# One streaming encoder step: the last whole gate chunks also go into pairs of half products

## The chip, the core and the metric

The kernel runs on one core of a Trainium2 chip. The metric is the device time of one launch in microseconds (us), as the median of three runs. The engines named below are TensorE (PE in the profile; PEld is its weight loads), VectorE (DVE), ScalarE (ACT), GpSimd (POOL) and SyncE (SP, which here only issues DMAs).

## What is computed

Two layers work on 640 tokens (512 of a prompt, 8 x 16 of running streams). Cut to what matters here, a layer is:

```
(a_u, a_v, a_g, b_x, b_g, c_q, c_kv, c_kr, c_g, m_q, gate_logits) = split_cols(x @ w_in)
oa = gmlp(a_u, a_v) * silu(a_g)              # branch A
ob = rglru(conv4(b_x)) * silu(b_g)           # branch B, a recurrence over the tokens
oc = mla(c_q, c_kv, c_kr) * silu(c_g)        # branch C
om = mem_attend(m_q, mem_k, mem_v)           # branch M
g = sigmoid(gate_logits).reshape(B, T, 4, D_MODEL)
merged = g[0]*(oa @ w_a) + g[1]*(ob @ w_b) + g[2]*(oc @ w_c) + g[3]*(om @ w_m)
x = layer_norm(ALPHA * x + merged @ w_out)
```

`gate_logits` has 4 x 1024 columns. With 128 columns to a chunk that is 32 gate chunks in each layer, eight for each branch.

## The kernel before

Every float32 operand of a product is split into a high and a low part (ACT casts the high one, DVE subtracts to get the low one), and a product takes three passes: high by high, high by low, low by high. There are two ways to compute a chunk of 128 columns of `x @ w_in` for all 640 tokens:

- **Whole** (`fm_chunk`, line 121 in the profile, tile `fm`): 8 blocks of the inner dimension x 3 passes x 2 halves of the tokens, 48 matmuls of 128x128 by 320.
- **In pairs** (`Pair`, `run_pair`, `product`, line 423, tiles `fp_a`, `fp_b`, `fp_c`): two chunks together are a 2x2 block product, done by a scheme with seven half products of 12 matmuls each, 84 in all. It needs sums of weight blocks (DVE, line 369), sums of blocks of x (the `xt` tiles, made early in the layer, put in DRAM and brought back by `x_sums_back`, line 356), and some additions of results (line 372). `on()` keeps the operations of the pairs in a fixed order on each engine.

A gate chunk is followed by tanh (ACT) and the branch's product `y` (`merge_y`, 24 matmuls, tile `y`, line 121), which DVE multiplies by the gate and adds to `macc`.

The recurrence of branch B is worked in four chunks c of 128 channels. For each: `lru_in(c)` (a whole chunk `fm`, its copy out of PSUM into `lb[c % 2]`, and a convolution on DVE, line 994), `lru_split(c)` (splits the result into the one tile `lx`, and loads and splits the gate weights `lru_w`), `lru_gates(c)` (12 matmuls, tile `gate`, line 1015, and two tanh) and `lru_rest(c)` (about ten dependent operations on DVE, ACT and POOL, with the scan on line 1036). There are only two `lb` buffers, so `lru_in(3)` can't copy its chunk out of PSUM until `lru_rest(1)` is done.

The end of a layer runs so: `lru_in` and `lru_gates(0)`, `lru_rest(0)` between the four steps of `mem_prompt` (branch M's attention, tiles `ms_ps`, `ptm_ps`, `mo_ps`); then `merge_whole` with the first four gate chunks of branch A, computed whole, written by hand between `lru_gates(1)` to `lru_rest(3)`; then `merge_pairs` with 14 pairs for the other 28 gate chunks; then the output projection (`y_ps`).

Buffers come from pools by tag, and all tiles of a tag share its slots. The ones at issue: `acc` in PSUM, **2** slots of two banks, used by `fm`, `gate`, `y` and `fp_a`; `raw`, 3 slots, every weight load; `t` (`tmp`), 5 slots, among others `tu` of a pair and `osrc` (the branches brought back from DRAM, line 1156, `Branch.back`); `f` (`ftmp`), 2 slots, `a2` of the recurrence, `z0` and `z1` of a pair; `o`, 10 slots, x, `xt`, `bhl`, `oa`, `um`. The framework makes the order of instructions on each engine from the order of the program text and from what is ready; the tiles of a pair may thus stand earlier on an engine than in the text, if they get their slots.

Of the kernel before, what the change touches and what calls it, by code (L numbers as in the profile page):

```python
# [11 lines left out]
AF = mybir.ActivationFunctionType  # L12
# [7 lines left out]
T = NP_ + NS  # L20
# [19 lines left out]
def encoder_step(  # L40
# [6 lines left out]
    PE, DVE, ACT, POOL = nc.tensor, nc.vector, nc.scalar, nc.gpsimd  # L47
# [26 lines left out]
    def ftmp(shape, name, dtype=F32):  # L74
        return tp.tile(shape, dtype, tag="f", name=name, bufs=2)
# [35 lines left out]
    def wload(src, n=1024):  # L111
        return whl(wraw(src, n), n)
# [67 lines left out]
    def halves(ap):  # L180
        return ap.rearrange("p (a b) -> p a b", a=2)
# [18 lines left out]
    for l in range(L):  # L200
# [91 lines left out]
        def fm_chunk(c, l=l):  # L292
            h, lo = wload(ins["w_fm"][l, c])
            o = acc("fm")
            fm_product(o, kcols(h), kcols(lo), xhk, xlk, KD)
            return o[:, :, 0:TH]
# [92 lines left out]
        class Pair:  # L389
            def __init__(self, c):  # L390
                self.c = c
# [166 lines left out]
        for t in range(NT):  # L558
            DVE.tensor_scalar(
                out=cb[:, t, 0:256], in0=cb[:, t, 0:256], scalar1=rs[:, 0, t:t + 1], scalar2=None, op0=ALU.mult,  # L560
            )
            DVE.scalar_tensor_tensor(
                out=cb[:, t, 256:384], in0=cb[:, t, 256:384], scalar=rs[:, 1, t:t + 1], in1=kv_g,
# [30 lines left out]
        for n in range(2):  # L594
# [11 lines left out]
            out=wm, in_=wm, pattern=[[0, 8], [1, 128]],  # L606
# [25 lines left out]
        for j, bank in ((0, bank_t), (1, bank_o)):  # L632
            o = trs(bank("cqT_ps"), [cb[:, t, j * 128:(j + 1) * 128] for t in range(4)])
            split(cqh[:, j, 0:NP_], cql[:, j, 0:NP_], o, q_g[:, j:j + 1])
        o = trs(
            bank_t("lat4_ps"), [cb[:, 4, 0:128], cb[:, 4, 128:256], cb[:, 4, 256:384], krp[:, 4, :]]
        )
# [3 lines left out]
        for r in (0, 64):  # L641
            DVE.tensor_copy(
                out=krT_s[r:r + 32, :, 128:144], in_=o[r:r + 32, 384:512].rearrange("p (b t) -> p b t", b=NB)
# [5 lines left out]
        for c in range(4):  # L649
            o = acc("mix").rearrange("p a b -> p (a b)")  # L650
            for t in range(NT):
                PE.matmul(
                    out=o[:, t * 128:(t + 1) * 128], lhsT=v[:, t, c * 128:(c + 1) * 128],
# [42 lines left out]
        for n in range(2):  # L696
            o = acc("q_ps")
# [302 lines left out]
        def lru_split(c):  # L1000
            split(xch, xcl, lb[c % 2][:, 1, 0:NXC])
            raw = wraw(ins["lru_w"][l, c], 256)
            wh = wp.tile([128, 256], F32R, tag="lwh", name="lwh", bufs=1)
            wl = wp.tile([128, 256], F32R, tag="lwl", name="lwl", bufs=1)
            split(wh, wl, raw)
            lw[c] = wh, wl

        def lru_gates(c):
            half = NXC // 2
            wh, wl = lw[c]  # L1010
            for m, dst in enumerate((lb[c % 2][:, 2, 0:NXC], lb[c % 2][:, 0, 0:NXC])):
                o = acc("gate")
                for n, (a, b) in enumerate(((wh, xch), (wl, xch), (wh, xcl))):
                    for j in range(2):
                        PE.matmul(
                            out=o[:, j, 0:half], lhsT=a[:, m * 128:(m + 1) * 128],
                            rhs=b[:, j * half:(j + 1) * half], start=(n == 0), stop=(n == 2),
                        )
                ACT.activation(
                    out=halves(dst), in_=o[:, :, 0:half], func=AF.Tanh, scale=0.5, bias=hb[:, m, c:c + 1]  # L1020
                )

        def lru_rest(c):
            i_, xc, r_ = (lb[c % 2][:, j, 0:NXC] for j in range(3))
            DVE.scalar_tensor_tensor(out=i_, in0=i_, scalar=1.0, in1=xc, op0=ALU.add, op1=ALU.mult)
            ACT.activation(out=xc, in_=r_, func=AF.Tanh, scale=sp4[:, c:c + 1], bias=sp4[:, c:c + 1])
            ACT.activation(out=r_, in_=r_, func=AF.Exp, scale=sn4[:, c:c + 1], bias=sn4[:, c:c + 1])
            a2 = ftmp([128, NXC], "a2")
            POOL.tensor_tensor(out=a2, in0=r_, in1=r_, op=ALU.mult)
            DVE.scalar_tensor_tensor(out=xc, in0=a2, scalar=1.0, in1=xc, op0=ALU.add, op1=ALU.mult)  # L1030
            ACT.activation(out=xc, in_=xc, func=AF.Sqrt, scale=0.25)
            DVE.tensor_tensor(out=i_, in0=i_, in1=xc, op=ALU.mult)
            rst = slice(XP - 1, XP - 1 + (NB - 1) * XB + 1, XB)
            POOL.memset(r_[:, rst], 0.0)
            POOL.tensor_copy(out=i_[:, rst], in_=h0[:, c, :])
            DVE.tensor_tensor_scan(out=xc, data0=r_, data1=i_, initial=0.0, op0=ALU.mult, op1=ALU.add)
            POOL.tensor_copy(out=lh[:, c, 0:1], in_=xc[:, NP_ - 1:NP_])
            POOL.tensor_copy(out=lh[:, c, 1:9], in_=xc[:, XP + TS - 1:XP + TS + (NB - 1) * XB:XB])
            DVE.tensor_tensor(out=ob[c][:, 0:NP_], in0=ob[c][:, 0:NP_], in1=xc[:, 0:NP_], op=ALU.mult)
            obs = ob[c][:, NP_:T].rearrange("p (b t) -> p b t", b=NB)  # L1040
            DVE.tensor_tensor(out=obs, in0=obs, in1=samp(lb[c % 2][:, 1, :])[:, :, 0:TS], op=ALU.mult)
            spill(1, c, ob[c])
# [53 lines left out]
        def bsplit(bi, get):  # L1096
            nk, scale = (2, 1.0) if bi == 3 else (4, 0.5)
            if bi == 3:
                t_ = otile([128, 2, nk, T], F32R, "bhl")
                bhl = [t_[:, 0], t_[:, 1]]  # L1100
            else:
                bhl = [otile([128, nk, T], F32R, f"bhl{j}") for j in range(2)]
            for k in range(nk):
                split(bhl[0][:, k, :], bhl[1][:, k, :], get(k), scale)
            return bhl

        def merge_y(bi, f, g, wh, wl, bhl):
            nk = 2 if bi == 3 else 4
            y = acc("y")
            fm_product(y, kcols(wh), kcols(wl), lambda k: bhl[0][:, k, :], lambda k: bhl[1][:, k, :], nk)  # L1110
            y = y[:, :, 0:TH]
            m = macc[:, f, :]
            o = m if bi == 0 else g
            DVE.scalar_tensor_tensor(
                out=halves(o), in0=halves(g), scalar=1.0, in1=y, op0=ALU.add, op1=ALU.mult
            )
            if bi > 0:
                DVE.tensor_tensor(out=m, in0=m, in1=g, op=ALU.add)
# [3 lines left out]
            for e in range(2):  # L1122
                split(mg[-1][:, 0, e, :], mg[-1][:, 1, e, :], macc[:, f + e, :], 0.5)

        def merge_whole():
            bhl = bsplit(0, lambda k: oa[:, k, :])
            for f in range(4):
                o = fm_chunk(22 + f)
                g = ftmp([128, T], "g")
                ACT.activation(out=halves(g), in_=o, func=AF.Tanh, scale=0.5)  # L1130
                wh, wl = wload(ins["w_br"][l, 0, f], 512)
                merge_y(0, f, g, wh, wl, bhl)
                yield bhl

        class Branch:
            def __init__(self, bi, f, bhl=None):
                self.bi, self.f, self.n = bi, f, 256 if bi == 3 else 512
                self.br = (0, 2, 1, 3)[bi]
                self.src = ins["w_brm"][l] if bi == 3 else ins["w_br"][l, self.br]

# [17 lines left out]

            def run(self, z):
                wh, wl = self.hl  # L1160
                if self.bi not in bhls:
                    bhls[self.bi] = bsplit(self.bi, self.back)
                for e in range(2):
                    c = slice(e * self.n, (e + 1) * self.n)
                    merge_y(self.bi, self.f + e, z[e], wh[:, c], wl[:, c], bhls[self.bi])

        bhls = {}

        def merge_pairs(bhl):
            bhls[0] = bhl  # L1170
            ys = [Branch(0, f) for f in (4, 6)] + [Branch(bi, f) for bi in (1, 2, 3) for f in (0, 2, 4, 6)]
            ps = [Pair(22 + y.br * 8 + y.f) for y in ys]
            first_pair(ps[0])
            for n, y in enumerate(ys):
                def act(e, cols, z, v_):
                    on("ACT", ACT.activation(out=z[:, cols], in_=v_, func=AF.Tanh, scale=0.5))  # L1176

                run_pair(ps[n], ps[n + 1] if n + 1 < len(ps) else None, act, y)
                if y.bi == 3 and y.f == 0:
                    merge_split(0)  # L1180
            for f in (2, 4, 6):
                merge_split(f)
# [11 lines left out]
        last = mem_prompt(3, last)  # L1194
        for c in range(2):
            spill(3, c, om[:, c, :])
        ma = merge_whole()
        bhl = next(ma)
        lru_gates(1)
        lru_rest(1)  # L1200
        lru_split(2)
        lru_in(3)
        next(ma)
        lru_gates(2)
        lru_rest(2)
        lru_split(3)
        next(ma)
        next(ma)
        lru_gates(3)
        lru_rest(3)  # L1210
        nc.gpsimd.dma_start(out=outs["lh"][l], in_=lh)
        x_sums_back()
        merge_pairs(bhl)


        wo = {}
# [187 lines left out]
```

## Time and profile before

| what | value |
|---|---|
| median of 3 runs | 1408.05 us (1407.63 to 1408.15) |
| profiled execution, its own time | 1407.16 us |
| its span, first to last instruction | 1405.5 us |
| mean granted clock of TensorE | 0.995 |
| instructions | 22592 |
| PE busy, PEld busy | 1367.4 us (97%), 1257.8 us (89%) |
| DVE, ACT, POOL busy | 986.3 us (70%), 645.5 us (46%), 122.7 us (9%) |

An engine is busy while one of its instructions runs. The profile also has the chain of waits (each piece is the work or the wait that released the next), a timeline of each engine, and busy time and granted clock by stretches. A timeline line has its start, its length, engine, line, operation, output and inputs, and in brackets the idle time before it and what ended that. Layer 0 goes to about 707 us, layer 1 from there.

### The profile page before, as it was taken

The page shows a single profiled execution, that of the slowest core. Times are in us where ns is not written, and L with a number is a line of the kernel's source. Part 1 is how long each engine was busy: PE and PEld are TensorE (multiplying, and loading weights), DVE is VectorE, ACT ScalarE, POOL GpSimd, SP SyncE. Part 2 cuts the span into 40 slices and gives each one's busy share as a digit, 9 for nine tenths or more (in the row PEclk, how much of TensorE's full clock was granted, in tenths as well). Part 3 has the DMA queues.
Part 4 walks back from the last instruction along what each step waited for, and adds up shares of the span by engine and source line. Part 5 has one row for each costly group of instructions (what it writes and reads, how often), then busy time and mean ns, then how long its engine had stood idle before and what let it go on. Part 6 is the DMA issues. An engine that isn't in the chain of part 4 may idle for free.

```text
span 1405.5 us, 22592 instructions
## 1 busy us (share of the span) xinstructions
PE 1367.4 (97%) x8896; PEld 1257.8 (89%) x8896; DVE 986.3 (70%) x1676; ACT 645.5 (46%) x1159; POOL 122.7 (9%) x254
## 2 busy tenths in 40 slices
PE   8999999999999999999999999999999999999997
PEld 8798888778999999998888889887799999999986
DVE  8667757676676676676885877576765676767765
ACT  6454544455554343454244535343655444434530
POOL 1100210022110000000112012000121100000000
PEclk9999999999999999999999999999999999999999
DMA  7724532164342223236375346231542433322443
GB/s 267 279 96 162 196 92 100 41 225 141 94 139 88 94 95 100 75 106 217 103 229 203 98 161 208 74 125 47 198 140 80 139 109 88 96 81 76 124 139 113
DMA packets 59098, 183.96 MB, mean 131 GB/s; under 512 B 6640, under 2 KB 15760, under 8 KB 55920
## 3 DMA queue, kind: packets, MB, share of 16 engines
q1 hardware_dynamic: 48304, 127.54, 28.3%
q0 software_dynamic: 10688, 54.98, 10.7%
q8 instruction: 70, 1.15, 0.3%
q14 instruction: 36, 0.29, 0.1%
HBM read 148.49 MB, written 32.69 MB: 129 GB/s over the span
## 4 chain that ended last, share of the span: by engine, by line
PE 80%; DVE 10%; DMA 4%; issue 3%; ACT 2%; POOL 0%; DVEq 0%; SPq 0%; ACTq 0%
PE fp_a L423 17%; PE y L121 13%; PE fm L121 13%; PE y_ps L1249 8%; PE fp_c L423 7%; PE fp_b L423 5%; PE sc_ps L837 3%; PE v L136 2%; DMA raw<-in_w_fm 2%; PE c L136 2%; PE pv_ps L861 2%; PE pt_ps L854 1%; DVE wl L384 1%; PE q_ps L121 1%; DVE wl L147 1%
## 5 line engine op out<-in xcount | busy, mean ns | idle before, releaser
L384 DVE TENSOR_TENSOR wl<-raw,wh 128x1024 fp32r<-128x1024 f32 (+1 forms) x148 | 154.9, 1048 | 56.3 <-PE fp_c L423 28.7
L379 ACT CAST wh<-raw 128x1024 fp32r<-128x1024 f32 (+1 forms) x148 | 134.9, 912 | 56.4 <-PE fp_c L423 34.6
L121 PE MATMUL y<-bhl,wh 128*128 128x320 f32 x896 | 142.9, 310 | 0.2 <-ACT z L1176 0.2
L121 PEld LDWEIGHTS y<-bhl,wh 128*128 128x128 f32 x896 | 134.0, 188 | 0.8 <-ACT z L1176 0.5
L121 PE MATMUL fm<-xl,wh 128*128 128x320 f32 x448 | 113.9, 327 | 0.0
L121 PE MATMUL fm<-xh,wh 128*128 128x320 f32 x448 | 112.6, 322 | 0.0
L423 PE MATMUL fp_c<-xt,wh 128*128 128x320 f32 x640 | 107.2, 309 | 1.4 <-ACT z L375 1.2
L423 PE MATMUL fp_a<-xt,wh 128*128 128x320 f32 x640 | 106.9, 309 | 0.0
L423 PE MATMUL fp_a<-xh,wh 128*128 128x320 f32 x320 | 98.1, 318 | 8.4 <-DVE z L372 7.9
L423 PEld LDWEIGHTS fp_c<-xt,wh 128*128 128x128 f32 x640 | 97.0, 188 | 2.2 <-ACT z L375 2.2
L423 PEld LDWEIGHTS fp_a<-xt,wh 128*128 128x128 f32 x640 | 97.2, 188 | 0.0
L423 PE MATMUL fp_a<-xl,wh 128*128 128x320 f32 x320 | 96.8, 314 | 0.0
L375 ACT COPY tu<-fp_a 128x320 f32<-128x320 f32 x80 | 34.0, 425 | 128.3 <-PE fp_a L423 126.7
L146 ACT CAST wh<-raw 128x1024 fp32r<-128x1024 f32 (+3 forms) x67 | 63.8, 953 | 57.5 <-PE fm L121 17.8
L147 DVE TENSOR_TENSOR wl<-raw,wh 128x1024 fp32r<-128x1024 f32 (+3 forms) x67 | 74.0, 1105 | 21.7 <-ACT wh L146 8.5
L121 PE MATMUL fm<-xh,wl 128*128 128x320 f32 x448 | 85.0, 324 | 0.0
L379 ACT CAST wh<-ws 128x1024 fp32r<-128x1024 f32 x40 | 41.9, 1047 | 90.7 <-DVE ws L369 90.7
L121 PEld LDWEIGHTS fm<-xl,wh 128*128 128x128 f32 x448 | 75.7, 188 | 8.3 <-issue 6.4
L121 PEld LDWEIGHTS fm<-xh,wh 128*128 128x128 f32 x448 | 75.6, 188 | 6.1 <-issue 5.3
L121 PE MATMUL y<-bhl,wl 128*128 128x320 f32 x448 | 76.1, 309 | 0.0
L121 PEld LDWEIGHTS fm<-xh,wl 128*128 128x128 f32 x448 | 67.9, 188 | 5.8 <-issue 5.1
L423 PEld LDWEIGHTS fp_a<-xh,wh 128*128 128x128 f32 x320 | 61.4, 192 | 11.8 <-DVE z L372 11.1
(346 smaller groups left out, 2979.3 us busy)
## 6 DMA issues: line engine op xcount, KB each, us to landing
raw<-in_w_fm SPq DMA_DIRECT2D x108, 512.0 KB, 3.6
xsum<-xt POOLq DMA_DIRECT2D x8, 1280.0 KB, 11.6
xt<-xsum POOLq DMA_DIRECT2D x8, 1280.0 KB, 6.3
raw<-in_w_br SPq DMA_DIRECT2D x20, 512.0 KB, 3.9
mcache<-in_mem_kv SPq DMA_DIRECT2D x8, 1024.0 KB, 6.7
raw<-in_w_out SPq DMA_DIRECT2D x16, 512.0 KB, 5.1
osrc<-oscr POOLq DMA_DIRECT2D x20, 320.0 KB, 3.3
gscr<-th POOLq DMA_DIRECT2D x16, 320.0 KB, 2.6
```

The source lines that it names most:

```text
L121: PE.matmul(out=out[:, j, 0:TH], lhsT=a(k), rhs=b(k)[:, j * TH:(j + 1) * TH], start=(n == 0), stop=(n == len(steps) - 1),)
L136: PE.matmul(out=o[:, 0:width], lhsT=a(ci * nk_per + j)[:, t * 128:(t + 1) * 128], rhs=w[:, j * width:(j + 1) * width], start=(ci == 0 and ...
L146: ACT.copy(out=dst_h, in_=src)
L147: DVE.tensor_tensor(out=dst_l, in0=src, in1=dst_h.bitcast(F32), op=ALU.subtract)
L375: on("ACT", ACT.copy(out=out, in_=in_))
L379: on("ACT", ACT.copy(out=h, in_=src))
L384: on("DVE", DVE.tensor_tensor(out=lo, in0=src, in1=h.bitcast(F32), op=ALU.subtract))
L423: on("PE", PE.matmul(out=o, lhsT=a[:, k0:k0 + 128], rhs=b[:, k, :], start=(first and n == 0), stop=(n == len(steps) - 1), skip_group_check ...
L837: PE.matmul(out=s[:, 0:nk], lhsT=qT[0:kr_, h, ts_], rhs=kT[h // 4][0:kr_, h % 4, 0:nk], start=True, stop=True,)
L854: PE.transpose(tps[:, k * 128:(k + 1) * 128], p[:, k * 128:(k + 1) * 128], ident)
L861: mm = PE.matmul(out=ops[64 * e:64 * e + 64, hp * 128:(hp + 1) * 128], lhsT=vc[:, k, h * 64:(h + 1) * 64], rhs=pt[:, k * 128:(k + 1) * 128 ...
L1249: PE.matmul(out=o[j], lhsT=mg[k // 2][:, a, k % 2, t * 128:(t + 1) * 128], rhs=wo[k, w][:, j * 512:(j + 1) * 512], start=(k == 0 and p == ...
```

## The change

The four whole gate chunks go. All 32 gate chunks are made in pairs, 16 in a layer instead of 14; the first two pairs are those of branch A, f = 0 and 2. `merge_whole` is gone, and with it its text between the steps of the recurrence; the split of `oa` stays where it was. The steps of the recurrence follow one another directly, `x_sums_back` and `merge_pairs` stand behind them as before. The loads of `w_br` for those four chunks become two loads of twice the size.

```diff
-        def merge_whole():
-            bhl = bsplit(0, lambda k: oa[:, k, :])
-            for f in range(4):
-                o = fm_chunk(22 + f)
-                g = ftmp([128, T], "g")
-                ACT.activation(out=halves(g), in_=o, func=AF.Tanh, scale=0.5)
-                wh, wl = wload(ins["w_br"][l, 0, f], 512)
-                merge_y(0, f, g, wh, wl, bhl)
-                yield bhl
-
...
-        def merge_pairs(bhl):
-            bhls[0] = bhl
-            ys = [Branch(0, f) for f in (4, 6)] + [Branch(bi, f) for bi in (1, 2, 3) for f in (0, 2, 4, 6)]
+        def merge_pairs(bhls):
+            ys = [Branch(bi, f, bhls) for bi in range(4) for f in (0, 2, 4, 6)]
             ps = [Pair(22 + y.br * 8 + y.f) for y in ys]
             first_pair(ps[0])
...
-        ma = merge_whole()
-        bhl = next(ma)
-        lru_gates(1)
-        lru_rest(1)
-        lru_split(2)
-        lru_in(3)
-        next(ma)
-        lru_gates(2)
-        lru_rest(2)
-        lru_split(3)
-        next(ma)
-        next(ma)
-        lru_gates(3)
-        lru_rest(3)
+        bhls = {0: bsplit(0, lambda k: oa[:, k, :])}
+        for c in (1, 2, 3):
+            lru_gates(c)
+            lru_rest(c)
+            if c < 3:
+                lru_split(c + 1)
+            if c == 1:
+                lru_in(3)
         nc.gpsimd.dma_start(out=outs["lh"][l], in_=lh)
         x_sums_back()
-        merge_pairs(bhl)
+        merge_pairs(bhls)
```

## Rows read from the trace of the kernel before

**Rows 1.** The page, part 1: busy time, share of the span, instructions.

```profile
PE 1367.4 (97%) x8896; PEld 1257.8 (89%) x8896; DVE 986.3 (70%) x1676; ACT 645.5 (46%) x1159; POOL 122.7 (9%) x254
```

**Rows 2.** Chain of waits, 300 to 420 us: start, length, what, matmuls.

```profile
362.58 7.04 PE fm L121 x48
...
399.25 7.04 PE y L121 x48
406.29 1.76 PE fp_a L423 x12
```

**Rows 3.** Stretches: length, busy time by engine, granted clock, DMA.

```profile
440.00:455.00 15.00, 15.00 (x105) 15.00 (x104) 9.05 (x12) 5.32 (x8) 0.00 (x0) 1.00 0.26 82
```

**Rows 4.** Timeline of PE around the recurrence, layer 0, and two lines of layer 1.

```profile
305.57 0.47 PE L1015 MATMUL gate<-lx,lwh 128*128 128x332 f32 x2
...
323.00 0.46 PE L121 MATMUL fm<-xh,wh 128*128 128x320 f32 x2
...
336.74 1.09 PE L1083 MATMUL mo_ps<-pt_m,mem 128*64 128x128 f32 x16
...
340.50 0.47 PE L1015 MATMUL gate<-lx,lwh 128*128 128x332 f32 x2
...
383.54 0.47 PE L1015 MATMUL gate<-lx,lwh 128*128 128x332 f32 x2
...
385.69 0.30 PE L423 MATMUL fp_a<-xh,wh 128*128 128x320 f32 x1
...
399.08 2.51 PE L121 MATMUL y<-bhl,wh 128*128 128x320 f32 x16
...
1038.22 0.47 PE L1015 MATMUL gate<-lx,lwh 128*128 128x332 f32 x2
...
1083.42 0.30 PE L423 MATMUL fp_a<-xh,wh 128*128 128x320 f32 x1
```

**Rows 5.** Timeline of POOL, its DMA issues that bring tiles back.

```profile
344.03 0.54 POOL L356 DMA_DIRECT2D xt<-xsum  x1 [4.38 <-DMA oscr<-um]
...
437.26 0.54 POOL L1156 DMA_DIRECT2D osrc<-oscr  x1 [18.82 <-ACT wh L379]
456.62 0.54 POOL L1156 DMA_DIRECT2D osrc<-oscr  x1 [18.82 <-ACT wh L379]
```

**Rows 6.** Timeline of SP: the load of the gate weights of c = 1.

```profile
260.68 0.33 SPq L103 DMA_DIRECT2D raw<-in_lru_w  x1
```

**Rows 7.** Timeline of ACT in the recurrence, layer 0.

```profile
311.58 0.43 ACT L146 CAST lwh<-raw 128x256 fp32r<-128x256 f32 x1
...
342.55 0.75 ACT L146 CAST lx<-lb 128x664 fp32r<-128x664 f32 x1
...
346.92 1.28 ACT L1031 ACT_TABLE_LOAD   x1
349.19 0.76 ACT L1031 ACTIVATE lb<-lb 128x664 f32<-128x664 f32 x1 [0.99 <-DVE lb L1030]
```

**Rows 8.** Timeline of DVE in the recurrence and after it, layer 0.

```profile
321.04 1.54 DVE L1036 TENSOR_TENSOR_SCAN lb<-lb 128x664 f32<-128x664 f32 x1 [0.29 <-POOL lb L1035]
...
343.33 0.85 DVE L147 TENSOR_TENSOR lx<-lb,lx 128x664 fp32r<-128x664 f32 x1 [0.61 <-ACT lx L146]
...
351.64 1.54 DVE L1036 TENSOR_TENSOR_SCAN lb<-lb 128x664 f32<-128x664 f32 x1 [0.30 <-POOL lb L1035]
...
355.05 2.81 DVE L994 SCALAR_TENSOR_TENSOR lb<-lb,vec 128x664 f32<-128x664 f32 x3
...
433.48 0.82 DVE L150 SCALAR_TENSOR_TENSOR bhl<-osrc,bhl 128x640 fp32r<-128x640 f32 x1
```

**Rows 9.** Stretches around a pause of PE earlier in layer 0.

```profile
140.00:144.00 4.00, 2.69 (x19) 2.43 (x17) 0.76 (x2) 0.58 (x1) 1.82 (x1) 1.00 0.52 189
146.00:149.00 3.00, 3.00 (x13) 3.00 (x12) 2.80 (x6) 2.11 (x3) 0.54 (x1) 0.50 0.00 0
```

**Rows 10.** Timeline of PE: the instruction that ends that pause.

```profile
145.08 0.41 PE L423 MATMUL fp_a<-xh,wh 128*128 128x320 f32 x1 [2.39 <-DVE z L372]
```

More of the change, by code (lines that the diff above doesn't have):

```diff
@@ L1123, in merge_split, with __init__ @@
                 split(mg[-1][:, 0, e, :], mg[-1][:, 1, e, :], macc[:, f + e, :], 0.5)
-        def merge_whole():
-            bhl = bsplit(0, lambda k: oa[:, k, :])
-            for f in range(4):
-                o = fm_chunk(22 + f)
-                g = ftmp([128, T], "g")
-                ACT.activation(out=halves(g), in_=o, func=AF.Tanh, scale=0.5)
-                wh, wl = wload(ins["w_br"][l, 0, f], 512)
-                merge_y(0, f, g, wh, wl, bhl)
-                yield bhl
         class Branch:
-            def __init__(self, bi, f, bhl=None):
-                self.bi, self.f, self.n = bi, f, 256 if bi == 3 else 512
+            def __init__(self, bi, f, bhls):
+                self.bi, self.f, self.n, self.bhls = bi, f, 256 if bi == 3 else 512, bhls
                 self.br = (0, 2, 1, 3)[bi]
@@ L1160, in run @@
                 wh, wl = self.hl
+                bhls = self.bhls
                 if self.bi not in bhls:
@@ L1165, in run @@
                     merge_y(self.bi, self.f + e, z[e], wh[:, c], wl[:, c], bhls[self.bi])
-        bhls = {}
-        def merge_pairs(bhl):
-            bhls[0] = bhl
-            ys = [Branch(0, f) for f in (4, 6)] + [Branch(bi, f) for bi in (1, 2, 3) for f in (0, 2, 4, 6)]
+        def merge_pairs(bhls):
+            ys = [Branch(bi, f, bhls) for bi in range(4) for f in (0, 2, 4, 6)]
             ps = [Pair(22 + y.br * 8 + y.f) for y in ys]
```

## The prediction, made before the change was run

> **What bounds the kernel now.** I read the shares first: PE is busy 97% of the span, far ahead of DVE at 70% [rows 1]. A share is an average, so next come the stretches. With pairs in a steady run PE and its weight loads are both busy 15.00 of 15 us, and DVE has 9.05, ACT 5.32 [rows 3]: there the time is the number of matmuls and nothing else. Then the chain of waits through the end of a layer: from gates(1) to the first pair it is almost only PE, the whole chunks at 7.04 us for 48 matmuls and two products y at the same price [rows 2], so a matmul costs 0.147 us. The timeline of PE shows what fills the time beside the recurrence: gates(1) begin at 340.50, gates(3) at 383.54, the first pair at 385.69 [rows 4]. Between, PE does `lru_in(3)`, three of the four whole gate chunks with their y and the gates, without a pause worth naming; the first whole chunk stood beside `mem_prompt`, from 323.00 [rows 4]. Layer 1 repeats layer 0: 45.20 us from gates(1) to the first pair against 45.19 [rows 4]. I sum one layer and double it.
>
> **What is removed and added on PE.** Two whole chunks are 2 x 7.04 = 14.08 us; a pair is 7 x 1.76 = 12.32 us [rows 2]; each pair saves 1.76 us. The y products keep their 24 matmuls each, so four new pairs in two layers save 4 x 1.76 = 7.04 us if PE stays full. A pair adds sums and splits on DVE and ACT, but a steady pair with its y (19.36 us) leaves DVE idle 40% of the time [rows 3], so they cost nothing there. Eight loads of `w_br` become four of twice the size: nothing on PE's path.
>
> **What is moved: whether the pairs can stand beside the recurrence.** In the text they come after `lru_rest(3)`. They can only be pulled ahead if `fp_a` gets one of two `acc` slots. So I asked in which order slots are given out. After pair 2 the four `osrc` slots of tag t are free, the last but one read at 433.48 [rows 8], and POOL idles 18.82 us, yet the next branch's four `osrc` loads go out one per pair, at 437.26, 456.62 and so on [rows 5], each when a pair has let go of its `tu`. The free slots are being kept for the `tu` of pairs to come, which stand earlier in the text. The weights of gates c = 1 were likewise loaded at 260.68 [rows 6] and first cast at 311.58 [rows 7], holding a slot of three for 50 us. So a tag's slots are given in the order of the text, ready or not. For `acc` the order after the change is: gates(1), `lru_in(3)`, gates(2), gates(3), then `fp_a` of the first pair. **The pairs then wait until gates(3) have run**, and nothing covers the recurrence any more. Waiting at the head of PE's queue is the first product; behind it stand all 16 pairs and their y, and for those the DVE and ACT work of the pairs.
>
> **How long that wait is.** The first pair can start 385.69 - 383.54 = 2.15 us after gates(3), when the first gate's slot is read out [rows 4]. Break-even is a start at 385.69 - 2 x 19.36 = 346.97 us, since two pairs with y must fit before the work that now starts at 385.69. The chain to gates(3):
> - gates(1) move to 323.00, in the place of the first whole gate chunk [rows 4].
> - gates to the end of the scan: 353.18 - 340.50 = 12.68 us when alone, 322.58 - 305.57 = 17.01 us for c = 0, which ran beside `mem_prompt` [rows 4, 8]. After the change c = 1 runs beside `mem_prompt`, so I take 17.01.
> - the end of the scan frees `lb[1]`; copy-out and convolution of c = 3 end 357.86 - 353.18 = 4.68 us later [rows 8].
> - the split of c = 3: cast and subtraction, 344.18 - 342.55 = 1.63 us [rows 7, 8].
> - c = 2's recurrence now runs on the same engines at the same time; one operation of 0.85 us in front of the split [rows 8] is my value, 0 to 3 us its bounds (a scan of 1.54 and another of its kind).
> - then 2.15 us.
>
> Sum: 323.00 + 17.01 + 4.68 + 1.63 + 0.85 + 2.15 = 349.32 us, 2.35 us past break-even. The same with 12.68 and no contention is 344.14, 2.83 us ahead of it.
>
> **Two smaller terms.** PE has in this time only `lru_in(3)`, the rest of `mem_prompt` and gates. It will stand still for several us before gates(3). Earlier in the layer a pause of 2.39 us [rows 10] in full clock was followed by a stretch at 0.50 (1.2 of 2.4 GHz), 3.00 us of it in the row [rows 9]: half of that, 1.5 us, is lost. I take one such stretch, bounds 0 and two (3.0). And the first pair beside `lru_rest(3)` took 399.08 - 385.69 = 13.39 us instead of 12.32 [rows 4], 1.07 us; that stays, and the tail of `lru_rest(2)` beside the same pair adds between 0 and another 1.07, I take 0.5.
>
> A layer: 2.35 + 1.5 + 0.5 = 4.35 us, two layers 8.7 us. The profiled execution took 1407.16 us for its span of 1405.5; 1407.16 + 8.7 = 1415.9. It lies 0.9 us under the median of the runs, so **1416.7 us** for the median.
>
> **Queues passed.** SP loads go in the order of the text, now lru_w(2), `lru_in(3)`, lru_w(3), then the first pair's two; the last waits for lru_w(2) to be read after gates(1), well before 340: no cost. POOL's fourth `xt` load is issued at 344.03, when `um` is written out [rows 5]; the product that reads it is the sixth, 8.8 us after the pair's start, so at 349 no cost, but it binds if pairs start early (below).
>
> **A table switch.** An ACT table load before the square root takes 1.28 us and ends at 348.20, 0.99 us before the input is there at 349.19 [rows 7]: hidden, and I charge nothing. The Trainium skill (ScalarE: Activation LUTs, What ACT_TABLE_LOAD costs) counts 1.28 us plus a drain of about 1.38 for each switch; by that the load would have ended at 349.58, later than the trace has the next instruction start, so the trace does not bear it out here; by the page the sum would be about 0.4 us higher per recurrence step on the chain.
>
> **Rivals.**
> 1. *Pairs do run beside the recurrence*, slots going to whoever is ready. Then PE stays full and the time falls: by all 7.04 us to 1401.0. [...] Against it, two more recurrence steps stand beside pairs, 1.07 us each, 4.3 us in two layers, to 1405.3; and a start soon after 337, when `mem_prompt` ends [rows 4], puts the sixth product at about 346, where the `xt` load issued at 344.03 [rows 5] may not have landed. I place it at 1403. The `osrc` rows speak against it; no row shows `acc` itself. Chance 0.20.
> 2. *The wait is there, but the chain is short*: 12.68 instead of 17.01, no contention. The start is 344.14; with clock and stall 2.83 - 2.0 = 0.8 us gained a layer, 1406.4; without them up to 5.7 us gained, 1402.4. For it: the last operation of `mem_prompt` on PE starts at 336.74 [rows 4], and from there the recurrence has DVE and ACT to itself. Chance 0.18.
> 3. *DVE and ACT become the bound* when two recurrence steps, the convolution and the first pair's sums meet: 17.01 with 3 us of contention (4.5 past break-even), two clock stretches (3.0) and 1.07: 8.6 us a layer, 1425. It decides where gates(3) start after about 349. Chance 0.10.
>
> The forecast itself, a wait that costs more than the pairs save, has 0.52.
>
> **How the numbers follow.** 1416.7 is the likeliest case; its own range, one bound at a time, is 1411 to 1422. The range for 8 in 10 leaves out the best of rivals 1 and 2 and the worst of rival 3: 1402.5 to 1425. Under 0.2% (2.8 us), about what a measurement of this kernel can tell from no change, I count as same. Faster: rival 1 with 0.16, rival 2 with 0.04, 0.20. Same: 0.04 of rival 1, 0.12 of rival 2, 0.02 of the forecast, 0.18. The rest, 0.62, is slower.
>
> **What would show it.** In the changed profile: the first `fp_a` of a layer after the last `gate`, at 349 or so in layer 0; PE idle by some us between the end of `lru_in(3)`'s matmuls and gates(3), released by DVE or ACT of the recurrence; gates(1) at 323; a stretch of clock 0.50 behind the pause; from the third pair on the same spacing as before. I'm wrong if `fp_a` stands ahead of gates(2), or if PE has no pause there.

## The result and the profile after

| what | before | after |
|---|---|---|
| median, runs of this comparison | 1408.1 us (1407.63 to 1409.98) | 1422.52 us (1421.6 to 1422.6) |
| ratio to before | 1 | 1.0107, 95% interval 1.0093 to 1.0121 |
| profiled execution, its own time | 1407.16 us | 1422.51 us |
| its span | 1405.5 us | 1420.8 us |
| mean granted clock of TensorE | 0.995 | 0.990 |
| instructions | 22592 | 22544 |

The change makes the kernel 14.4 us slower. The engines' busy times, page part 1 (share of the span, instructions):

```profile
PE 1363.6 (96%) x8848; PEld 1255.7 (88%) x8848; DVE 1008.1 (71%) x1708; ACT 655.1 (46%) x1179; POOL 126.6 (9%) x254
```

PE has 48 matmuls fewer than in [rows 1] and is busy 3.8 us less, in a span 15.3 us longer. So the loss is time in which PE stands still. The timeline of PE shows where:

```profile
306.44 0.46 PE L1015 MATMUL gate<-lx,lwh 128*128 128x332 f32 x2
...
323.86 0.46 PE L1015 MATMUL gate<-lx,lwh 128*128 128x332 f32 x2
...
341.97 0.47 PE L1015 MATMUL gate<-lx,lwh 128*128 128x332 f32 x2
349.38 0.92 PE L1015 MATMUL gate<-lx,lwh 128*128 128x332 f32 x2 [6.94 <-ACT lx L146]
...
352.87 0.47 PE L423 MATMUL fp_a<-xh,wh 128*128 128x320 f32 x1
...
364.62 1.44 PE L423 MATMUL fp_c<-xt,wh 128*128 128x320 f32 x8 [1.19 <-ACT z L375]
...
376.04 0.31 PE L423 MATMUL fp_a<-xh,wh 128*128 128x320 f32 x1
...
395.40 0.31 PE L423 MATMUL fp_a<-xh,wh 128*128 128x320 f32 x1
...
1011.90 0.76 PE L1015 MATMUL gate<-lx,lwh 128*128 128x332 f32 x2
...
1101.09 0.31 PE L423 MATMUL fp_a<-xh,wh 128*128 128x320 f32 x1
```

The rows answer [rows 4]. Gates(1) are at 323.86, gates(3) at 349.38 behind a pause of 6.94 us, and only then comes the first `fp_a`, at 352.87. The third pair, the one that is first in the kernel before, starts at 395.40. I count from the start of gates(0), since executions are shifted against one another there by up to 4 us: the third pair starts 395.40 - 306.44 = 88.96 us after gates(0), before 385.69 - 305.57 = 80.12 [rows 4]. That is 8.84 us later, of which 1.07 come back, since the pair in that place no longer has a step of the recurrence beside it: 7.77. In layer 1 it is 1101.09 - 1011.90 = 89.19 against 1083.42 - 1003.20 = 80.22 before, 8.97 and net 7.90. Together 15.7 us; the spans differ by 15.3. Gates(0) of layer 1 in the trace of before:

```profile
1003.20 0.46 PE L1015 MATMUL gate<-lx,lwh 128*128 128x332 f32 x2
```

The chain of waits of after through the same stretch (start, length, what ran):

```profile
334.43 3.67 DMA raw<-in_w_fm
...
338.12 0.69 DVE ws L369
338.81 0.77 DVE lb L1032
...
341.73 0.67 DVE ws L369
...
344.92 1.22 DVE wl L384
346.14 0.82 DVE lb L994
346.96 0.77 DVE lb L1025
347.75 0.94 ACT lb L1026
348.69 0.65 ACT lx L146
349.38 2.04 PE gate L1015 x6
...
359.75 0.95 ACT lb L1027
...
366.77 0.47 DVE z L372
367.29 2.02 PE fp_a L423 x12
369.31 6.89 PE y L121 x47
```

In [rows 2] this chain is only PE. Now it comes through the load of the first pair's weights (334.43) and then runs on DVE, ACT and POOL from 338 to 367: first the end of `lru_rest(1)` and the convolution of chunk 3, mixed with the first pair's sums (`ws`, line 369) and its subtraction (`wl`, line 384), then gates(3), `lru_rest(2)` and `lru_rest(3)` (line 1027 at 359.75), whose scan is followed by the pair's `z`. PE is on it for some 2 us. From `y` at 369.31 on, it is PE again. Stretches of after (length, then busy time by engine, granted clock, share and rate of DMA):

```profile
342.00:349.00 7.00, 0.44 (x3) 0.17 (x2) 6.70 (x10) 3.85 (x8) 4.73 (x10) 0.73 0.50 164
349.00:352.00 3.00, 2.62 (x9) 2.62 (x10) 1.27 (x2) 1.73 (x3) 1.40 (x2) 0.50 0.91 372
352.00:356.00 4.00, 4.00 (x18) 4.00 (x18) 1.78 (x3) 3.94 (x5) 0.20 (x1) 0.57 0.38 139
```

In the pause DVE is busy 6.70 of 7 us. Behind it PE runs at half clock (0.50) for all of gates(3) and nearly all of the first product.

### The profile page after: what moved, and what is told of

Same layout as the page of the kernel before. It is cut to its first block, busy times and chain, and to the rows that moved or that the text cites. A ratio compares the mean times of both kernels' runs of the same rounds, so it can differ in the third digit from the quotient of the medians.

```text
span 1420.8 us, 22544 instructions
## 1 busy us (share of the span) xinstructions
PE 1363.6 (96%) x8848; PEld 1255.7 (88%) x8848; DVE 1008.1 (71%) x1708; ACT 655.1 (46%) x1179; POOL 126.6 (9%) x254
## 4 chain that ended last, share of the span: by engine, by line
PE 81%; DVE 9%; DMA 4%; issue 2%; ACT 2%; POOL 1%; DVEq 0%; SPq 0%; ACTq 0%
PE fp_a L423 19%; PE y L121 14%; PE fm L121 8%; PE fp_c L423 8%; PE y_ps L1231 8%; PE fp_b L423 5%; PE c L136 3%; DMA raw<-in_w_fm 3%; PE sc_ps L837 3%; PE v L136 2%; PE pv_ps L861 2%; DVE wl L384 1%; PE pt_ps L854 1%; PE q_ps L121 1%; PE mem L136 1%
## 5 line engine op out<-in xcount | busy, mean ns | idle before, releaser
L384 DVE TENSOR_TENSOR wl<-raw,wh 128x1024 fp32r<-128x1024 f32 (+1 forms) x164 | 172.4, 1052 | 53.2 <-PE fp_c L423 34.2
L379 ACT CAST wh<-raw 128x1024 fp32r<-128x1024 f32 (+1 forms) x164 | 150.0, 915 | 60.9 <-PE fp_c L423 41.0
L121 PE MATMUL fm<-xl,wh 128*128 128x320 f32 x320 | 84.1, 333 | 0.0
L121 PE MATMUL fm<-xh,wh 128*128 128x320 f32 x320 | 84.0, 329 | 0.0
L146 ACT CAST wh<-raw 128x1024 fp32r<-128x1024 f32 (+3 forms) x51 | 50.5, 990 | 58.1 <-PE fm L121 13.9
L147 DVE TENSOR_TENSOR wl<-raw,wh 128x1024 fp32r<-128x1024 f32 (+3 forms) x51 | 58.7, 1152 | 20.1 <-ACT wh L146 9.2
L369 DVE TENSOR_TENSOR ws<-raw 128x512 f32<-128x512 f32 x88 | 60.5, 688 | 15.4 <-DMA raw<-in_w_fm 14.6
L121 PEld LDWEIGHTS y<-bhl,wl 128*128 128x128 f32 x448 | 68.3, 188 | 0.0
L423 PEld LDWEIGHTS fp_a<-xl,wh 128*128 128x128 f32 x352 | 67.3, 191 | 0.1
L423 PE MATMUL fp_a<-xh,wl 128*128 128x320 f32 x352 | 66.6, 312 | 0.0
```

Source lines behind the costliest of these rows:

```text
L121: PE.matmul(out=out[:, j, 0:TH], lhsT=a(k), rhs=b(k)[:, j * TH:(j + 1) * TH], start=(n == 0), stop=(n == len(steps) - 1),)
L146: ACT.copy(out=dst_h, in_=src)
L147: DVE.tensor_tensor(out=dst_l, in0=src, in1=dst_h.bitcast(F32), op=ALU.subtract)
L369: on("DVE", DVE.tensor_tensor(out=out, in0=x, in1=y, op=ALU.add))
L379: on("ACT", ACT.copy(out=h, in_=src))
L384: on("DVE", DVE.tensor_tensor(out=lo, in0=src, in1=h.bitcast(F32), op=ALU.subtract))
```

## The experiments

The twelve runs, with the distance from the start of gates(0) in layer 0 to the first `fp_a` and to the third pair (the pair f = 4 of branch A, which all kernels have). Ratios are to the kernel before on the same chip; its medians there were 1406.4 to 1406.5 us.

| kernel | median us | ratio, 95% interval | to first fp_a | to third pair |
|---|---|---|---|---|
| b0_before | 1404.41 | 0.9988 (0.9977 to 0.9999) | 80.13 | 80.13 |
| e0_after | 1421.53 | 1.0103 (1.0090 to 1.0116) | 46.28 | 88.83 |
| e1_bank | 1422.69 | 1.0117 (1.0100 to 1.0134) | 35.82 | 87.71 |
| e2_bank_z | 1416.68 | 1.0068 (1.0055 to 1.0081) | 35.83 | 85.36 |
| e3_between | 1420.40 | 1.0097 (1.0083 to 1.0110) | 31.69 | 85.60 |
| e4_whole_last | 1422.94 | 1.0113 (1.0099 to 1.0128) | 87.52 | 87.52 |
| e5_half | 1403.30 | 0.9972 (0.9960 to 0.9983) | 57.32 | 80.08 |
| e6_no_xt4 | 1405.21 | 0.9993 (0.9981 to 1.0006) | 31.68 | 79.58 |
| e7_clock | 1420.83 | 1.0101 (1.0088 to 1.0114) | 45.21 | 88.24 |
| e8_hold | 1423.58 | 1.0120 (1.0107 to 1.0133) | 46.14 | 89.81 |
| e9_no_table | 1418.95 | 1.0099 (1.0084 to 1.0113) | 48.39 | 88.23 |
| e10_half_last | 1410.58 | 1.0044 (1.0027 to 1.0061) | 62.25 | 85.79 |

Two of them are yardsticks, the kernels before and after without an edit.

> The kernel before, unedited, run as the others of this group are, for its trace on the same chip and for what a comparison of a kernel with itself gives: ratio 1.000, within 0.0015 to either side.

> The changed kernel itself, unedited, beside the kernels of this group on the same chip: 1.0107 of the kernel before again (1.009 to 1.012). Both theories say the same; it is the measure for the other three.

The kernel before against itself came out at 0.9988: a ratio within about 0.0015 of 1 says nothing here. The changed kernel repeated its loss.

**Is it the place in the text, or the pairs?** e4 keeps all four whole chunks and moves only their text:

```diff
-        bhl = next(ma)
+        bhl = bsplit(0, lambda k: oa[:, k, :])
         lru_gates(1)
...
         lru_split(3)
-        next(ma)
-        next(ma)
         lru_gates(3)
         lru_rest(3)
+        for _ in merge_whole(bhl):
+            pass
```

> The kernel before, with its four whole gate chunks and 14 pairs kept and only their place in the text moved: the split of oa where it is, the chunks behind lru_rest(3), as the pairs stand in the changed kernel. My theory: the first fm of a whole gate chunk waits in acc for gates(3), PE stands still for 4 to 7 us before gates(3), half clock behind it; the first of them starts at 350 to 353 in layer 0, then 4 x (7.04 + 3.52) = 42.24 us to the first pair, at 392.5 to 396 instead of 385.69: 7 to 10 us a layer, 1422 to 1428 us, slower than before without one more pair. Rival (the pairs' own work costs the time, not the place in the text): 1408 to 1411.

PE of e4, where the first whole gate chunk now starts:

```profile
347.08 0.92 PE L1015 MATMUL gate<-lx,lwh 128*128 128x332 f32 x2 [5.06 <-ACT lx L146]
...
350.37 0.46 PE L121 MATMUL fm<-xh,wh 128*128 128x320 f32 x2
```

1.0113, as slow as the changed kernel, without one more pair. The pause, the gates at half clock, and the first chunk right behind gates(3): the place in the text alone makes a loss of that size, and the matmuls that the pairs save don't show beside it (the intervals of e4 and e0 overlap).

**Is it the slot of acc?** e1 gives the first pair's `fp_a` (`own` is true for that pair alone) another bank and moves nothing:

```diff
-            ba = acc("fp_a")[:, 0, 0:TH]
+            ba = bank_o("fp_a")[:, 0:TH] if own else acc("fp_a")[:, 0, 0:TH]
```

> The changed kernel, but the first pair of each layer's merge takes its fp_a from the one bank of tag o in PSUM (last used by mo_ps) in place of a slot of acc. The order of the text stays. My theory (slots of acc given out in the order of the text, so fp_a waits for the last gates): the first fp_a of layer 0 starts at about 341.5 instead of 352.87, when mo_ps is read out (341.47 in the changed kernel), and three to four products stand ahead of gates(3), PE's pause of 6.94 us is mostly gone. But z1 of that pair takes a slot of tag f behind a2 of rest(3), again by the order of the text, so the pair comes to a stop in front of its sixth product until about 363: its first y at 365 to 368 instead of 369.15, a gain of 1 to 4 us a layer, 1415 to 1420 us. Rival (the work of the pair on DVE and ACT beside the recurrence is what costs the time, whoever has the slots): the early start pushes gates(3) back by as much as it fills, 1422 or more. Rival (the slots are not it): first fp_a stays after gates(3), 1422.5.

e2 also takes the pair's results out of the slots that the recurrence's `a2` uses:

```diff
-            z0, z1, t_ = ftmp([128, T], "z0"), ftmp([128, T], "z1"), tmp([128, T], "tu")
+            t_ = tmp([128, T], "tu")
+            z0, z1 = ((tmp if own else ftmp)([128, T], n) for n in ("z0", "z1"))
```

> As the kernel with fp_a in its own bank, and besides the first pair's z0 and z1 from tag t instead of tag f, so that neither waits for a2 of the recurrence. My theory: first fp_a at about 341.5 in layer 0, no stop behind it, the first y at 358 to 361 instead of 369.15; 8 to 10 us gained a layer against the changed kernel, 1402 to 1407 us, faster than before (1408.1) with the text's order of pairs untouched. Rival (work of pairs on DVE and ACT beside the recurrence): 1415 or more. Rival (slots are not it): 1422.5.

PE of e1: the start of the pair, and its stop:

```profile
339.57 0.30 PE L423 MATMUL fp_a<-xh,wh 128*128 128x320 f32 x1
...
346.63 0.58 PE L1015 MATMUL gate<-lx,lwh 128*128 128x332 f32 x2 [0.89 <-ACT lx L146]
...
356.73 2.50 PE L423 MATMUL fp_a<-xt,wh 128*128 128x320 f32 x8 [6.97 <-ACT tu L375]
```

The first part is settled: with its own bank `fp_a` starts behind gates(2), 10.5 us sooner after gates(0), with nothing else moved, and gates(3) don't suffer (42.88 us after gates(0), 42.94 in after). So `acc` was what held it. But the gain isn't there: four products run, the fourth among gates(3), then PE waits 6.97 us for `tu`. I expected the stop one product later and a gain of 1 to 4 us a layer; the third pair is 1.12 us sooner than in e0, and the ratio doesn't show it. e2 shares neither slot with the recurrence and still stops, at the sixth product, for 5.25 us. ACT of e2 says for what:

```profile
349.16 1.52 ACT L1020 ACTIVATE lb<-gate,vec 128x664 f32<-128x664 f32 x2 [1.10 <-PE gate L1016]
350.69 1.28 ACT L1032 ACT_TABLE_LOAD   x1
...
352.76 1.28 ACT L1027 ACT_TABLE_LOAD   x1
354.06 0.94 ACT L1027 ACTIVATE lb<-lb,nl 128x664 f32<-128x664 f32 x1
354.90 0.60 ACT L379 CAST wh<-raw 128x512 fp32r<-128x512 f32 x1
...
356.26 0.40 ACT L375 COPY z<-fp_c 128x320 f32<-128x320 f32 x1
```

The pair's cast (line 379) had its input at 348.98, the copy of `z` its own soon after, and both stand in ACT's queue behind the square root of `lru_rest(2)`, the tanh of `lru_rest(3)` and two table loads. My theory counted slots alone; the order of work on ACT holds the pair up as well. e2 gains 3.47 us on e0 at the third pair, not 8 to 10, and stays slower than before: its 1416.68 us is what the rival had expected, 1415 or more.

**Can the text put it right?** e3 has no new buffer, only the steps in another order:

```diff
+        pairs = merge_pairs(bhls)
         lru_gates(1)
...
         lru_in(3)
+        x_sums_back()
+        next(pairs)
         lru_gates(2)
         lru_rest(2)
         lru_split(3)
+        next(pairs)
         lru_gates(3)
```

> The changed kernel with the text in another order and nothing else: the first pair stands between lru_in(3) and gates(2), the second between lru_split(3) and gates(3), as the whole chunks did; all fp_a from acc, all z from f. My theory: slots come in the new order, so the first fp_a of layer 0 starts before gates(2), near 338, PE has no pause over 2 us up to gates(3), and the two layers gain what the matmuls save less some stalls: 1408.1 - 7.04 = 1401.1 to 1405.4 (1.07 us for each of two recurrence steps beside pairs in two layers). Rival (DVE and ACT work of pairs beside the recurrence is the cost): two pairs are now beside three steps of it, 1415 or more. Rival (pairs in place of whole chunks save nothing here): 1408.

PE of e3, and then a part of its chain of waits:

```profile
335.38 0.31 PE L423 MATMUL fp_a<-xh,wh 128*128 128x320 f32 x1
...
354.65 1.98 PE L423 MATMUL fp_c<-xt,wh 128*128 128x320 f32 x8 [3.66 <-DMA xt<-xsum]
```

```profile
342.50 0.29 ACT um L1089
...
343.07 2.93 DMA oscr<-um
346.00 1.60 issue
347.60 7.00 DMA xt<-xsum
```

The order did what I said: the first pair starts 31.69 us after gates(0), ahead of gates(2). And the time stayed, at 1.0097. The new wait is the fourth `xt` tile. Its buffer is that of `um`; branch M's last output is copied at 342.50, written out until 346.00, and the load then takes 7.00 us. The prediction had named this load and left it, since at 349 it cost nothing. e6 is e3 with that load out of the first pair's way: the first pair reads the third sum of x again and leaves the fourth out (`x4` is 3 for it and 4 for the others):

```diff
-            product(bc, w2, 1, 4, False, True)
+            product(bc, w2, 1, x4, False, True)
```

> The kernel with the pairs' text between the steps of the recurrence (e3_between), but the first pair of each layer reads the third sum of x again where it would read the fourth, so that it doesn't wait for the load of the fourth; that leaves the fourth sum out of the first pair. Everything else as there. Theory (what was left of the loss there is that load: it can be issued only when branch M's output has left its buffer, and PE stood still 3.66 us in layer 0 and ran 3.9 us at half clock behind it): the first pair's sixth product follows without that pause; 5 to 5.6 us a layer, 1409 to 1411 us, ratio 1.002 to 1.004. Rival (the pairs' work on DVE and ACT beside the recurrence is the cost there): ratio 1.008 or more, the pause only moves to another releaser.

0.9993, more than I had asked for: the load was the whole loss of e3. By the third pair it is 6.02 us in layer 0 (85.60 to 79.58) and 8.99 us in layer 1 (89.34 to 80.35), where e3 waits 6.65 us for it. It also shows how little there was to win. With the first two pairs beside the recurrence, the third pair comes 80.13 - 79.58 = 0.55 us sooner than before in layer 0 and 80.35 - 80.18 = 0.17 us later in layer 1, where the matmuls save 3.52 in each. The waits of PE in e6 between 320 and 345, beside `mem_prompt`, come to 0.65 + 0.22 + 0.32 + 0.66 + 0.68 + 0.58 + 0.51 = 3.62 us. In b0 they are 0.28 + 0.37 = 0.65: there the first whole gate chunk stands ahead of gates(1), and its 48 matmuls need nothing but weights and x. In e6 only the last of the seven waits, 0.51 us, is the pair's own, for `tu`. The others are waits of gates(1) and of `mem_prompt`, and the first four of them, 1.85 us, come before the pair has started (337.26). No run puts a pair ahead of gates(1), so what that place would give is open.

**The terms of the sum.** e7 fills the pause with 42 matmuls of 128x128 by 320 behind gates(2), on data that are there and with a result that isn't used:

```diff
             lru_gates(c)
+            if c == 2:
+                idle(lw["last"], 42)
             lru_rest(c)
```

> The changed kernel with 42 matmuls added behind gates(2) in each layer, whose result nobody reads, to fill PE's pause of 6.94 us in front of gates(3): 42 x 0.147 = 6.2 us, so they end before gates(3) can start. Nothing else is added or moved. Theory (the pause brings half clock, and half clock is a cost of its own beside the wait): no stretch at 0.50 from gates(3) on, from the start of gates(3) to the first fp_a 2.15 us instead of 3.49, and the first pair's first product at full clock, 1.2 us more; 1.3 to 2.7 us a layer, 3 to 5 us in all against the changed kernel. Rival (the pair waits for ACT and DVE of the recurrence anyway, so that what the clock costs is hidden behind those waits): 0 to 1 us in all, the third product of the pair still starts at about 361 minus nothing.

```profile
339.60 6.32 PE L1026 MATMUL idle<-xh 128*128 128x320 f32 x42
346.62 0.57 PE L1015 MATMUL gate<-lx,lwh 128*128 128x332 f32 x2 [0.70 <-ACT lx L146]
...
354.43 1.44 PE L423 MATMUL fp_a<-xt,wh 128*128 128x320 f32 x8 [1.67 <-ACT tu L375]
```

No half clock, and gates(3) to `fp_a` takes 2.36 us instead of 3.48. Then the third product waits 1.67 us for `tu`, and at the third pair 0.59 us are left of it in layer 0 and 0.22 in layer 1, and nothing in the ratio (1.0101 and 1.0103). The rival was right: the half clock is there, but nearly all of it is hidden.

e8 holds the pair's sums on DVE until chunk 3 is split (`hold` is the subtraction of `lru_split(3)`):

```diff
             p.low0()
+            if hold is not None:
+                tail["DVE"] = hold
             p.sums(0)
```

> The changed kernel with the first pair's three sums, the cast and the subtraction for its second weights held on DVE until the split of the recurrence's chunk 3 has run (an order on DVE alone; no wait is added on another engine). Theory (work of the pair stands between steps of the recurrence on DVE, and so delays gates(3): three sums of 0.69 us and one subtraction of 1.22 us between 338 and 346 in the changed kernel): gates(3) 1.2 to 2.5 us earlier after gates(0) than in the changed kernel (42.94 us there in layer 0), 2 to 5 us in all if the pair doesn't then wait for its sums. Rival (the recurrence's own chain on ACT and POOL sets the time, DVE has room): gates(3) at the same distance, total the same.

PE, then DVE and POOL of e8:

```profile
345.44 0.92 PE L1017 MATMUL gate<-lx,lwh 128*128 128x332 f32 x2 [5.26 <-ACT lx L146]
...
347.93 1.48 PE L1017 MATMUL gate<-lx,lwh 128*128 128x332 f32 x4 [1.01 <-DVE lx L147]
```

```profile
345.42 2.46 DVE L147 TENSOR_TENSOR lx<-lb,lx 128x664 fp32r<-128x664 f32 x1 [0.81 <-ACT lx L146]
```

```profile
345.85 1.30 POOL L1031 TENSOR_TENSOR a<-lb 128x664 f32<-128x664 f32 x1
```

Gates(3) start 41.27 us after gates(0), 1.53 sooner than in e0 (42.80): that is what the pair's work on DVE costs the chain. But the subtraction of the split now stands beside POOL's multiplication and takes 2.46 us instead of 0.85, the rest of gates(3) waits for it, and the first pair takes 374.62 - 350.31 = 24.31 us instead of 23.19: the third pair is 0.98 us later than in e0. Here, work that was moved out of one place on DVE was paid for in another.

e9 leaves out the recurrence's square root, and with it the switches of ACT's table:

```diff
-            ACT.activation(out=xc, in_=xc, func=AF.Sqrt, scale=0.25)
+            ACT.activation(out=xc, in_=xc, func=AF.Copy, scale=0.25)
```

> The changed kernel with the square root of the recurrence left out: the same ACT instruction of the same size as a scaled copy, so that ACT needs no table load for it and none to go back to tanh. Theory (the first pair's stalls come from standing behind the recurrence on ACT, and the table loads, 1.28 us each, two for each step, are a good part of that queue): the waits of PE in the first pair for tu and z (0.2, 1.19 and 0.5 us in the changed kernel's layer 0) shrink, gates(3) stand where they stood; 0.8 to 2 us a layer, ratio 1.0075 to 1.0095 beside 1.0103 for the changed kernel. Rival (the chain through DVE and POOL sets those waits): ratio 1.010 or more.

The first pair's length, start to start of the second, is 373.40 - 352.92 = 20.48 us in e9 and 372.45 - 349.26 = 23.19 in e0, and of its waits only one of 0.40 us is left. But the edit moved more than the table loads: on DVE the operations of the convolution and the recurrence fell in another order, and `lru_rest(2)` got out of the pair's way. Its scan in e9, and then in e0:

```profile
351.33 1.54 DVE L1036 TENSOR_TENSOR_SCAN lb<-lb 128x664 f32<-128x664 f32 x1 [0.29 <-POOL lb L1035]
```

```profile
351.91 1.54 DVE L1036 TENSOR_TENSOR_SCAN lb<-lb 128x664 f32<-128x664 f32 x1 [0.29 <-POOL lb L1035]
```

It starts 1.59 us before the first `fp_a` in e9 and 2.65 us after it in e0. So the 2.71 us are the table loads and a step of the recurrence that moved, and e9 can't tell them apart. In the total nothing shows: e9's first `fp_a` is 2.1 us later after gates(0). As a price of the table loads e9 is inconclusive.

**How much cover does it take?** e5 keeps two whole chunks (f = 0 and 1), in their old places, and puts one of 15 pairs where the other two stood. In e10 `x_sums_back` and all pairs stand behind `lru_rest(3)`; the rest is as here:

```diff
+        whole, pairs = merge_whole(bhls[0]), merge_pairs(bhls)
+        next(whole)
         lru_gates(1)
...
         lru_in(3)
+        next(whole)
         lru_gates(2)
         lru_rest(2)
         lru_split(3)
+        x_sums_back()
+        next(pairs)
         lru_gates(3)
```

> Half of the change with the place in the text kept: the first two gate chunks of a layer stay whole and stand where they stood in the kernel before (ahead of gates(1), and between lru_in(3) and gates(2)); the third and fourth, which stood between lru_split(3) and gates(3), become a pair in the same place; 15 pairs in a layer. Theory (slots in the order of the text; the fourth xt tile is there by 355 and the pair needs it later): PE full beside the recurrence as before, first fp_a of layer 0 before gates(3); one pair's 1.76 us gained a layer, less 0 to 1.07 us for one more step of the recurrence beside a pair: 1.4 to 3.5 us in all faster than before, ratio 0.9975 to 0.999. Rival (a pair beside the recurrence always costs more than it saves, by its work on DVE and ACT): ratio 1.001 or more.

> As e5_half (two whole chunks in their old places, 15 pairs), but all pairs stand in the text behind lru_rest(3), as in the changed kernel; so only the two whole chunks cover the recurrence. Theory (what costs is the uncovered chain from gates(1) to gates(3), and how much of it is uncovered decides, not the place in the text as such): gates(1) at 339.6 and gates(2) at 359.4 as in e5_half, gates(3) follow gates(2) by the split alone, at about 363, first fp_a at 365 to 366, a pause of 1 to 2 us and no half clock; first pair with two steps of the recurrence beside it, 2.4 us of stalls: 0.5 to 3 us in all over e5_half, ratio 0.998 to 1.0005. Rival (text order behind rest(3) costs as much here as in the changed kernel, 8.8 us a layer before the pairs' saving): ratio 1.006 or more.

PE of e10:

```profile
361.46 0.88 PE L1015 MATMUL gate<-lx,lwh 128*128 128x332 f32 x4 [1.53 <-ACT lwh L146]
...
364.75 0.42 PE L423 MATMUL fp_a<-xh,wh 128*128 128x320 f32 x1 [0.83 <-ACT lb L1019]
...
370.10 1.44 PE L423 MATMUL fp_a<-xt,wh 128*128 128x320 f32 x8 [1.54 <-ACT tu L375]
```

e5, at 0.9972, is the lowest of the edited versions. I claim little for it: the kernel before against itself gave 0.9988, and by the traces e5 is 0.05 us ahead at the third pair of layer 0 and 0.9 us in the span (1401.6 against b0's 1402.5). The 1.76 us that its pair saves a layer go into stalls: from its first `fp_a` at 362.01 to the next pair at 384.77, with gates(3) between, it takes 22.76 us; 19.36 for the pair and 2.09 for the gates leave 1.31. Another 0.51 us is a wait inside gates(2), for the slot of the whole chunk's `y`, that b0 doesn't have.

e10 fell between my theory and its rival. The uncovered wait is short as I said, but the first pair has `lru_rest(2)` and `lru_rest(3)` both beside it and takes 388.29 - 364.75 = 23.54 us, 4.18 over 19.36. In e5, where each of two pairs has one step beside it, the stalls are 1.31 and 1.07. Two steps of the recurrence beside one pair cost 4.18 us here, and 2.38 us spread over two.

## Why the prediction was right, and where its sum was not

The forecast was 1416.7 us, slower; 1422.52 was measured. The direction and the mechanism held, the size was 5.8 us short. The range that the forecast gives itself, 1411 to 1422 "one bound at a time", doesn't follow from its terms: moved one at a time, the bounds of contention, clock and stall give 1413.7 to 1421.0, and 1411 needs all the low ones together. The measured time lies above both, inside the wider range of 1402.5 to 1425.

- **The order of the slots**: right, and shown by e1 on `acc` itself. The first `fp_a` came after the last gates, gates(1) at 323.86 (forecast 323), the pause and the half clock were there, and from the second pair on the spacing is 19.36 us as before.
- **Rival 1**, pairs beside the recurrence at 1403: not what happened, and too hopeful where it was made to happen. e3 lost as much to the load of the fourth `xt` as the change lost to `acc`, and e6, without that load, ended at a ratio of 0.9993, where 1403 would be 0.9964.
- **The start of the first pair**: forecast 2.35 us past break-even, measured 46.43 - (80.12 - 38.72) = 5.03. Gates(1) to the end of scan 1: 341.81 - 323.86 = 17.95, forecast 17.01. Scan to the end of the convolution: 6.73, forecast 4.68. From there to gates(3): 0.84, since the gates begin on the cast alone, forecast 1.63 + 0.85. Together 1.34 us too little. The mis-sized term is the contention: I took one operation of 0.85 us; on DVE, in the chain of waits above, the pair's subtraction (`wl`, 1.22) and an operation of `lru_rest(2)` (line 1025, 0.77) stand among the steps of the convolution. I had counted the recurrence's own operations and not the first pair's sums and subtractions, which need no slot of `acc` and so came early. e8 puts them at 1.53 us. The queue that the prediction passed at no cost has a part in it: the pair's second load went out only when lru_w(2) had been read (334.36), its sum (`ws`) started at 338.12 when the load had landed, and the operation of `lru_rest(1)` behind it on DVE (line 1032) started 1.05 us after its input was there (337.68). In e8, with the sums out of the way, the end of that scan comes only 0.28 us sooner after gates(1) than in e0 (17.49 to 17.77), since a copy on POOL is then the last to come.
- **Gates(3) to the first pair**: 3.49 us, forecast 2.15, by the half clock. I had put the clock into a term of its own, 1.5 us.
- **The first pair**: 376.04 - 352.87 = 23.17 us; over 19.36 and the 1.07 that before has too, 2.74 remain, where the terms for clock and stall gave 2.0. The step that failed is which of them. e7 shows that the clock is nearly all hidden (0.59 us at the third pair), e9 that the stall goes when the table loads go and `lru_rest(2)` is out of the way (2.71 us; the two aren't separated). The prediction charged the clock 1.5, the stall 0.5 and a table switch nothing: I had looked at one switch that was hidden [rows 7]. In after six loads stand between 335 and 368; one of them, on ACT:

```profile
352.28 1.28 ACT L1031 ACT_TABLE_LOAD   x1
353.57 0.76 ACT L1031 ACTIVATE lb<-lb 128x664 f32<-128x664 f32 x1
```

  The load takes 1.28 us, as the Trainium skill has it (ScalarE: Activation LUTs, What ACT_TABLE_LOAD costs); the further 1.38 us of drain that it names is not in these rows, where the next instruction starts 0.01 us after the load has ended.
- **The sum**: 1.34 + 1.34 + 0.74 = 3.42 us a layer more than the 4.35 of the forecast, 7.77. **Rival 3** had DVE and ACT as the bound and 1425. The chain of waits of after is on those two from 338 to 367, so it was nearer to the mechanism behind gates(3) than my forecast, which ended the chain with the first pair's start, and nearer in size too.

What stays open: how much of the first pair's stall the table loads are, and why the instructions of the pair stand behind those of the recurrence on ACT in e1 and e2, though ready. That the order of the text decides there too is argued, not shown; e3 moved the text and the slots at once.

## What to carry to other kernels

Work that covers a dependent chain has to get its buffers ahead of the chain's last step; where slots are given in the order of the text, moving that work behind the chain in the text uncovers the chain. Slots of its own were not enough here: the work then stood behind the chain on ACT. Fewer instructions on the busiest engine gain only what the cover doesn't lose: with a whole chunk ahead of gates(1) PE waited 0.65 us beside `mem_prompt` (b0), without it 3.62 (e6), and no order tried here had the 7.04 us of saved matmuls in full. When a cover goes, follow the chain to where the busiest engine takes over again, count every operation of the moved work that needs none of the scarce slots, and count the operations and table loads of both users where two alternate on ACT.

## What the runs showed of the hardware

DVE's subtraction of 128x664 took 2.46 us beside a multiplication of 1.30 us on POOL (e8) and 0.85 us where POOL had none (after, 349.36): longer than the two one after the other. A DMA issue on POOL stood just ahead of that multiplication (345.30, 0.54 us), and the subtraction ended 0.73 us after the multiplication did; whether it waited for both isn't shown. Behind a pause of 6.94 us TensorE ran at half clock for about 6 us (after, 349.4 to 355.7), where behind the pause of 2.39 us before it was one stretch of some 3 us [rows 9, 10]; behind the 1.53, 0.83 and 1.54 us of e10 the granted clock stayed at 1.00. The length of a pause didn't settle it: behind one of 2.38 us in e10 (until 843.71) and one of 2.24 us in e7 (until 144.75) the granted clock stayed at 1.00 as well, so the pause of 2.39 us, from which the prediction took its half-clock stretch, shows what can follow such a pause and not what must.
